# Products on constants around the router and in the first stretch, and new offsets for the order of issue, in a hybrid attention and MoE layer

## The chip, the cores and the metric

The kernel runs on one core of one Trainium2 chip. The metric is the device time in microseconds (us) of one execution. The engines are named as in the profile: PE is TensorE's matmul, PEld its weight load, DVE VectorE, ACT ScalarE, POOL GpSimd, SP SyncE. A name with a q at its end (SPq, ACTq) is the sequencer of that engine where it issues DMAs.

## The reference

One layer of a decoder trunk is computed for 256 tokens of a prompt and for 8 sample sequences with one new token each, all in fp32. The 264 rows are called tokens below.

```python
sh1, sc1, g1, sh2, sc2, g2 = split(silu(c) @ ada_w + ada_b, 6)     # adaLN
h = rms_norm(x, norm1_w) * (1 + sc1) + sh1
z = h @ w_in                       # retention q k v g, attention q k v, indexer q k w
ret_out, ret_state = retention_group(...)        # 8 heads, chunks of 128
att_out = attend(...)              # sparse attention: indexer picks the top keys
x = x + g1 * (concat(ret_out, att_out) @ w_out)
h = rms_norm(x, norm2_w) * (1 + sc2) + sh2
logits = h @ router_w + router_b   # top 4 of 32 experts, softmax over the four
for e in 32 experts:
    hh = h @ w_gate_up[e] + b_gate_up[e]
    gate, up = min(hh[:, :1024], 7), clip(hh[:, 1024:], -7, 7)
    acc += combine[:, e] * (((up + 1) * gate * sigmoid(1.702 * gate)) @ w_down[e] + b_down[e])
x = x + g2 * acc
```

The outputs are the new x of both groups, the new keys, values and indexer keys, and the retention states. The experts' weights are 32 x 12.6 MB; they are by far most of what the kernel reads.

## The kernel before

**The stages.** The program is written as one function. First come the adaLN products (`ada_half`, line 319, and `ada_part`), the statistics of the first norm (line 390) and the scaling of the transposed input (`modulate`, line 401). Then the blocks of w_in are multiplied (line 536 for the prompt, 539 for the sample sequences), and retention and sparse attention are worked out between them. Then comes the projection w_out with the second norm (`norm2`, with transposes at line 268), the router (`router`, products at lines 1340 and 1342), the rank of each token in its expert's list (`ranks`, products at lines 1361 and 1362), the gathers of the first experts' tokens as products with one-hot matrices (`gather_in`, line 1378), and the 32 experts (gate and up at line 1564, down at line 1574).

**The weights.** All large weights go through one queue, SP's (`load`, line 165), in the order in which they are used, into a ring of tiles that holds 21 MB. A tile is loaded again when the last product that reads it is done. When the attention is over, the ring holds the first experts' weights, and the next load waits for expert 0's first four of eight gate and up pieces.

**The order.** Each part of the program is a segment (`seg`). The table `PRIO` gives a segment an offset in the scheduler's priority; the scheduler then puts the instructions of each engine into one fixed order. Segments without an entry stand as written. In each engine the instructions are issued in this order, and one that waits holds up those behind it. `chain()` ties instructions into a given order without a wait between engines.

**The products on constants.** Lines 281 to 283 multiply a 128x128 matrix of ones in bf16 with a broadcast of it, 128x512, twenty times at the start, before the first real product has data. Their result is read by nobody.

**Places that the prediction speaks of.** `ada_half(0)` ends with an addition on DVE (line 327) that the two transposes of `modulate` (line 268) wait for. In the middle stretch, lines 730 and 733 find the threshold of the top keys, line 776 (DVE) and 778 (PE) the row numbers of the keys that are gathered by POOL (line 893), lines 1043 and 1058 the softmax of the prompt's attention, and lines 302, 351 and 1081 fold the second norm's weight (`norm2_w`) into adaLN's rows and transpose them. ACT's queue issues the load of `norm2_w` (line 302), DVE multiplies (line 351), PE transposes (line 1081).

Of the kernel before, what the change touches and what calls it, by code (L numbers as in the profile page):

```python
# [11 lines left out]
F32 = mybir.dt.float32  # L12
# [17 lines left out]

WARM = 20

PRIO = {
# [12 lines left out]
}  # L46


# [70 lines left out]
def hybrid_step(ctx, tc, A, L, O, KP, KT, DEC, poff, toff, dbg=None, stop=None):  # L119
    nc = tc.nc  # L120
    dbg = dbg or {}
    V, S, G, T = nc.vector, nc.scalar, nc.gpsimd, nc.tensor
# [9 lines left out]
    def seg(name):  # L132

        if cur[0] is not None:
            cur[0].__exit__(None, None, None)
        o = PRIO.get(name)
        cur[0] = None
        if o is not None:
            cur[0] = tc.high_priority(offset=o)
            cur[0].__enter__()  # L140
# [125 lines left out]
    def transpose(out, in_):  # L266
        k = in_.shape[0]
        return T.transpose(out, in_, ident[:k, :k])
# [10 lines left out]
    S.dma_start(cr, L["c"])  # L279

    idle = thp()
    for i in range(WARM):
        T.matmul(idle.rearrange("p (n m) -> p n m", n=4), ones_b, ones_b[:, None, :].to_broadcast([128, 4, 128]), start=True, stop=True)

    sw_ = pe.tile([128, 204], F32, name="sw_")
    S.dma_start(sw_, L["small"])
# [34 lines left out]
    def ada_half(h, w):  # L321
        pa = acc()
        for k in range(8):
            for j in range(4):
                T.matmul(pa[32 * j:32 * j + 32, :256], cT[:, k, :], w[k][:, 256 * j:256 * j + 256], start=(k == 0), stop=(k == 7))
        sl = slice(256 * h, 256 * h + 256)
        V.tensor_add(ada[:, 0, sl], pa[:, :256], bias0[:, sl])

# [73 lines left out]
    def modulate(h):  # L402

        seg(f"AB{h}")
        pt = trp()
        for v in range(2):
            transpose(pt[:, 128 * v:128 * v + 128], ada[:, 0, 256 * h + 128 * v:256 * h + 128 * v + 128])
        ptv = pt[:, :256].rearrange("p (v s u r) -> p v s u r", v=2, s=2, u=2)
        qs = slice(2 * h, 2 * h + 2)
        V.tensor_copy(AB[:, qs, 0:64], pt[:, :256].rearrange("p (v m) -> p v m", v=2)[:, :, 0:64])  # L410
        for u in range(2):
            V.scalar_tensor_tensor(Av[:, qs, 1, u], ptv[:, :, 1, u], 1.0,
                                   n1T[:, 4 * h + 2 * u:4 * h + 2 * u + 2, None].to_broadcast([128, 2, 32]), op0=ALU.add, op1=ALU.mult)
        for i in range(4):
            k, u, q = 4 * h + i, i // 2, 2 * h + i % 2
            a_, b_ = AB[:, q, 64 + 32 * u:65 + 32 * u], AB[:, q, 32 * u:32 * u + 1]
            if i % 3 == 1:
                S.activation(hT[:, k, 0:256], hT[:, k, 0:256], AF.Identity, scale=a_, bias=b_)
            else:
                V.tensor_scalar(hT[:, k, 0:256], hT[:, k, 0:256], a_, b_, op0=ALU.mult, op1=ALU.add)  # L420
        hs = hT[:, 4 * h:4 * h + 4, 256:264].rearrange("p (u v) t -> p u v t", u=2)
        for i, op in ((1, ALU.mult), (0, ALU.add)):
            ins = G.tensor_tensor(hs, hs, Av[:, qs, i, :, 1:9].rearrange("p v u r -> p u v r"), op=op)
        if h == 0:
            pool1(ins)
# [7 lines left out]
    gidx = pe.tile([128, 4], I32, name="gidx")  # L433
    V.tensor_copy(gidx, ptf[:, 0:4])
    ikv = A["cache_idx_k"][0].rearrange("n (g k) d -> (n g) (k d)", g=8)
    seg("ikg")
    ikg = []
    for g in range(4):
# [27 lines left out]
    pe1 = chain()  # L466
# [822 lines left out]
    def norm2(c):  # L1289
# [20 lines left out]
        for n in range(2):  # L1310
            sl = slice(512 * n, 512 * n + 512)
            pt = trp()
            for k in range(4):
                transpose(pt[:, 128 * k:128 * k + 128], x[:, c, 512 * n + 128 * k:512 * n + 128 * k + 128])
            o = xT[:, 4 * n:4 * n + 4, 128 * c:128 * c + 128]
            if n:
                V.tensor_copy(o, pt.rearrange("p (k t) -> p k t", k=4))
            else:
                S.activation(o, pt.rearrange("p (k t) -> p k t", k=4), AF.Copy)
            S.activation(hn[:, c, sl], x[:, c, sl], AF.Square, accum_out=ss[:, n:n + 1])  # L1320
# [4 lines left out]
    def norm_rows(c):  # L1325
        seg(f'nr{c}')
        V.tensor_scalar(hn[:, c, 0:512], x[:, c, 0:512], rinv[:, c:c + 1], None, op0=ALU.mult)
        S.activation(hn[:, c, 512:], x[:, c, 512:], AF.Copy, scale=rinv[:, c:c + 1])
# [2 lines left out]
    G.memset(lx, 0.0)  # L1331
    G.memset(selb, 0.0)

    def router(c):
        seg(f'ro{c}')
        rows = 128 if c < 2 else 8
        pl = trp()
        for k in range(8):
            if c < 2:
                T.matmul(pl[:, 0:32], xT[:, k, 128 * c:128 * c + 128], rwm[:, k], start=(k == 0), stop=(k == 7))  # L1340
            else:
                T.matmul(pl[:8, 0:32], h2Ts[:, k], rw_[:, k], start=(k == 0), stop=(k == 7))
        lg = prep.tile([128, 2, NE], F32, name="lg", bufs=3)
# [79 lines left out]
    pr = smp()  # L1423
    ranks(0)
    norm_rows(0)
    norm2(1)
    seg("g0")
    oh0 = [prep.tile([128, D if n == "g1b" else 128], F32, name=n)[:, :112].rearrange("p (x t) -> p x t", x=2) for n in ("ones_f", "g1b")]
    px0 = [slots() for _ in range(2)]
    slot_hits(oh0[0], rankm[:, 0, 0:2])  # L1430
    for g in range(2):
        gather_in(px0[g], oh0[0], 0, g)
    router(1)
    ranks(1)
    norm_rows(1)
    seg("g1")
    slot_hits(oh0[1], rankm[:, 1, 0:2])
    for g in range(2):
        gather_in(px0[g], oh0[1], 1, g)
    seg("smx")  # L1440

    mx = prep.tile([128, 2, 3], F32, name="mx")
# [334 lines left out]
```

## Time and profile before

| | us |
|---|---|
| median of 3 runs | 1259.63 |
| fastest and slowest of them | 1259.60, 1273.12 |
| the profiled execution | 1265.59 |
| its span, first to last instruction | 1263.8 |
| mean granted TensorE clock | 0.977 |
| PE busy | 1177.6 (93%) |
| moved by DMA | 475.81 MB, 454.04 MB of it by the queue of the weights |

A granted clock of 1.00 is TensorE's 2.4 GHz, 0.50 its 1.2 GHz; these are the two levels. In a row of the timeline the first number is the start in us, the second the time that the group took, then engine, line, operation and tiles, the count, and in brackets how long the engine stood idle before it and what released it. In a row of windows stand a stretch, its length, the busy time of each engine with its count, the granted clock, the busy share of the 16 DMA engines, and GB/s.

### The profile page before, as it was taken

The numbers are of one execution on the slowest core, as the hardware profiler recorded it, in microseconds if no ns is written. First come the engines' busy times: TensorE is split into PE (matmuls) and PEld (weight loads), VectorE is DVE, ScalarE is ACT, GpSimd is POOL, SyncE is SP. The second block draws the span as 40 slices with busy tenths as digits, with TensorE's granted clock in tenths as the row PEclk, the third lists the DMA queues.
The fourth block names the chain that finished last, engine by engine and source line by source line (L and its number), as shares of the span: only waits on it lengthen the run. The fifth ranks groups of instructions, "written<-read, shape, count | busy, mean of one in ns | idle before, by whom it ended". The sixth has DMA issues, their size and how long they took to land. (4 is left out here: it accounts for less than half of the span.)

```text
span 1263.8 us, 14203 instructions
## 1 busy us (share of the span) xinstructions
PE 1177.6 (93%) x5661; PEld 471.6 (37%) x5662; DVE 489.3 (39%) x1171; ACT 134.6 (11%) x289; POOL 139.1 (11%) x221
## 2 busy tenths in 40 slices
PE   7999989889999999999999898989999898989898
PEld 3343333356643333433333333333333333333332
DVE  3339865436434333432334233323323332333243
ACT  1222112211210000000000000000000000000000
POOL 3402273340000000000000000000000000000000
PEclk8999999989899999999999999999999999999999
DMA  9636896757769999999999999999999999999997
GB/s 381 266 127 238 296 370 227 236 195 310 305 248 424 430 429 428 429 430 427 431 428 430 429 427 429 431 428 428 429 430 428 430 429 430 427 430 406 428 428 313
DMA packets 53350, 475.81 MB, mean 376 GB/s; under 512 B 6896, under 2 KB 7568, under 8 KB 15520
## 3 DMA queue, kind: packets, MB, share of 16 engines
q1 hardware_dynamic: 45472, 454.04, 85.9%
q0 software_dynamic: 4432, 13.74, 3.0%
q10 hardware_dynamic: 3376, 7.09, 1.9%
q8 instruction: 46, 0.75, 0.2%
q14 instruction: 24, 0.20, 0.0%
HBM read 470.69 MB, written 4.11 MB: 376 GB/s over the span
## 5 line engine op out<-in xcount | busy, mean ns | idle before, releaser
L1564 PE MATMUL pg<-w,xg 128*64 128x512 f32 x2048 | 471.9, 601 | 36.0 <-DMA w<-lay_w_exp 35.4
L1564 PEld LDWEIGHTS pg<-w,xg 128*64 128x64 f32 x2048 | 140.8, 137 | 324.3 <-issue 267.8
L1574 PE MATMUL py<-w,sg 128*64 128x512 f32 x1024 | 234.2, 599 | 12.0 <-DMA w<-lay_w_exp 11.5
L1538 DVE TENSOR_TENSOR hb<-pt,biasT 128x512 f32<-128x512 f32 x64 | 44.3, 692 | 358.1 <-PE pt L1497 349.4
L1523 POOL TENSOR_SCALAR og<-kp,rankm,comb 128x64 f32<-128x64 f32 (+1 forms) x64 | 36.7, 590 | 849.6 <-PE pz L1508 795.2
L1574 PEld LDWEIGHTS py<-w,sg 128*64 128x64 f32 x1024 | 70.8, 137 | 146.4 <-issue 129.2
L1530 ACT ACTIVATE hs<-pg 128x512 f32<-128x512 f32 x64 | 38.2, 597 | 619.9 <-PE pg L1564 619.9
L536 PE MATMUL acc<-w,hT 128*128 128x512 f32 x208 | 103.3, 628 | 0.2 <-DMA w<-lay_w_in 0.2
L1581 DVE TENSOR_TENSOR ys<-py,g2n 64x512 f32<-64x512 f32 x62 | 42.7, 689 | 113.2 <-PE py L1574 112.4
L1508 PE MATMUL pz<-ys,og 128*128 128x512 f32 (+1 forms) x136 | 68.1, 633 | 1.6 <-DVE ys L1577 0.8
L1511 DVE TENSOR_TENSOR x<-x,pz 128x512 f32<-128x512 f32 x68 | 46.5, 687 | 57.3 <-PE pz L1508 57.3
L1378 PE MATMUL pz<-oh,hn 128*128 128x112 f32 x480 | 58.1, 274 | 0.0
L1378 PEld LDWEIGHTS pz<-oh,hn 128*128 128x128 f32 x480 | 56.0, 192 | 0.0
L536 PEld LDWEIGHTS acc<-w,hT 128*128 128x128 f32 x208 | 37.2, 194 | 43.3 <-issue 41.1
L1543 ACT ACTIVATE sg<-hb 128x256 f32<-128x256 f32 x64 | 26.7, 417 | 223.1 <-DVE hb L1542 223.1
L1497 PEld LDWEIGHTS pt<-ident,hs 128*128 128x128 f32 x256 | 26.8, 140 | 52.3 <-issue 52.3
L1497 PE MATMUL pt<-ident,hs 128*128 128x128 f32 x256 | 42.0, 286 | 0.0
L1508 PEld LDWEIGHTS pz<-ys,og 128*128 128x128 f32 (+1 forms) x136 | 23.2, 192 | 46.1 <-issue 29.7
L1560 DVE COPY og<-pt 128x256 f32<-128x256 f32 (+1 forms) x17 | 7.2, 424 | 66.6 <-PE pt L1497 66.6
L1546 DVE TENSOR_TENSOR sg<-sg,hb 128x256 f32<-128x256 f32 x64 | 26.9, 421 | 3.9 <-DVE hb L1545 0.5
L1545 DVE SCALAR_TENSOR_TENSOR hb<-hb 128x256 f32<-128x256 f32 x64 | 27.2, 425 | 2.2
L314 PE MATMUL acc<-w,cT 128*32 128x512 f32 x128 | 25.9, 632 | 0.5 <-ACT t L846 0.5
(459 smaller groups left out, 858.4 us busy)
## 6 DMA issues: line engine op xcount, KB each, us to landing
w<-lay_w_exp SPq DMA_DIRECT2D x130, 2048.0 KB
w<-lay_w_exp SPq DMA_DIRECT2D x122, 1024.0 KB
w<-lay_ada_w SPq DMA_DIRECT2D x20, 1024.0 KB
w<-lay_w_in SPq DMA_DIRECT2D x15, 1024.0 KB
w<-lay_w_out SPq DMA_DIRECT2D x4, 1024.0 KB
s<-qd ACTq DMA_DIRECT2D x4, 512.0 KB
w<-lay_w_exp SPq DMA_DIRECT2D x4, 512.0 KB
hT<-lay_x SPq DMA_DIRECT2D x1, 1152.0 KB
```

The costliest lines, as they stand in the source:

```text
L536: T.matmul(pc[c], hT[:, k, 128 * c:128 * c + 128], w[k], start=(k == 0), stop=(k == 7))
L1378: put(T.matmul(px[:, k, :n, 8:64], hn[:, c, 512 * g + 128 * k:512 * g + 128 * k + 128], oh, start=(c == 0 and k == 0), stop=(c == 1 and k ...
L1497: on_pe(T.transpose(out, in_, ident[:k, :k]))
L1508: on_pe(T.matmul(pz[n], gT[i, 128 * c:128 * c + 128], ys[i, o:o + 512], start=True, stop=True))
L1511: V.tensor_add(x[:, c, sl], x[:, c, sl], pz[n])
L1523: G.tensor_scalar(og[:, c, js], iota2[:, 0:js.stop - js.start], rank(c), gate(c), op0=ALU.is_equal, op1=ALU.mult)
L1530: S.activation(hss[h], pg[h], AF.Copy)
L1538: V.tensor_tensor(hb, pt.rearrange("p (q b t) -> p q b t", q=4, b=2), bias.rearrange("p (b h q) -> p h q b", b=2, h=2)[:, h, :, :, None].t ...
L1545: V.scalar_tensor_tensor(up, up, 1.0, gate_, op0=ALU.add, op1=ALU.mult)
L1564: on_pe(T.matmul(pg[h][64 * b:64 * b + 64, :], xg[:, k, :], w[u][:, 512 * b:512 * b + 512], start=(k == 0), stop=(k == 7)))
L1574: on_pe(T.matmul(py[64 * n:64 * n + 64, :], sgs[k // 4][:, k % 4], w[u][:, 512 * n:512 * n + 512], start=(k == 0), stop=(k == 7)))
L1581: V.tensor_mul(ys[i64, 512 * n:512 * n + 512], py[64 * n:64 * n + 64], g2n[64 * n:64 * n + 64])
```

## The change

The change adds 25 products on constants, each of the form of lines 281 to 283: nine behind the products of `ada_half(0)` and five behind the two transposes of `modulate(0)`, both bound into one chain (`pe0`) with the work around them; and eleven (3, 3, 3 and 2) around the router and the gathers, bound by a chain `pe2` with the transposes of `norm2(1)`, the router's products and the gathers' products. It writes `router(1)` ahead of the first gather. And it gives new offsets to 35 segments in `PRIO`.

```diff
+WARM2 = (3, 3, 3, 2)
 PRIO = {
-    "AB": -400, "AB0": -1600, "AB1": 200, "Sst": 800, "ada0_0": 100, "ada0_1": 0, "ada1_0": -400, "ada1_5": 100, "ada2_0": -800,
+    "AB": -400, "AB0": -1600, "AB1": 200, "Sst": 800, "ada0_0": -100, "ada0_1": 1600, "ada1_0": -400, "ada1_5": 100,
...
     idle = thp()
-    for i in range(WARM):
-        T.matmul(idle.rearrange("p (n m) -> p n m", n=4), ones_b, ones_b[:, None, :].to_broadcast([128, 4, 128]), start=True, stop=True)
+    pe0 = chain()
+
+    def keep_busy(n):
+        for i in range(n):
+            pe0(T.matmul(idle.rearrange("p (n m) -> p n m", n=4), ones_b, ones_b[:, None, :].to_broadcast([128, 4, 128]), start=True, stop=True))
+
+    keep_busy(WARM)
...
+        if h == 0:
+            pe0(ins)
+            seg("wm")
+            keep_busy(9)
...
+            ins = transpose(pt[:, 128 * v:128 * v + 128], ada[:, 0, 256 * h + 128 * v:256 * h + 128 * v + 128])
+            if h == 0:
+                pe0(ins)
...
+    seg("wm")
+    keep_busy(5)
     seg("ikg")
...
+                if c:
+                    pe2(ins)
...
+    pe2 = chain()
+
+    def keep_warm(n, c):
+
+        seg(f"wm{c}")
+        t = pm_.tile([128, 512], F32, name="py")
+        for i in range(n):
+            pe2(T.matmul(t.rearrange("p (n m) -> p n m", n=4), ones_b, ones_b[:, None, :].to_broadcast([128, 4, 128]), start=True, stop=True))
...
-                T.matmul(pl[:, 0:32], xT[:, k, 128 * c:128 * c + 128], rwm[:, k], start=(k == 0), stop=(k == 7))
+                pe2(T.matmul(pl[:, 0:32], xT[:, k, 128 * c:128 * c + 128], rwm[:, k], start=(k == 0), stop=(k == 7)))
...
     norm_rows(0)
+    keep_warm(WARM2[0], 0)
     norm2(1)
+    keep_warm(WARM2[1], 1)
+    router(1)
+    keep_warm(WARM2[2], 2)
     seg("g0")
...
-        gather_in(px0[g], oh0[0], 0, g)
-    router(1)
+        gather_in(px0[g], oh0[0], 0, g, pe2)
+    keep_warm(WARM2[3], 3)
     ranks(1)
...
-        gather_in(px0[g], oh0[1], 1, g)
+        gather_in(px0[g], oh0[1], 1, g, pe2)
```

**PE, from the router to the first expert.** `pt<-rw_,h2Ts` is the router of the sample sequences, `pt<-rwp,mixT` that of the prompt (both halves), `pt<-ident,x` the transposes of `norm2(1)`, `pg<-selb,tri_b` and `pg<-selb,ones_b` the ranks, `pz<-...,hn` the gathers. Before:

```order
L1342 MATMUL pt<-rw__2344,h2Ts 8x32
L1340 MATMUL pt<-rwp,mixT 128x32 x8
L1342 MATMUL pt<-rw__2344,h2Ts 8x32 x7
L268 MATMUL pt<-ident,x 128x128 x8
L1362 LDWEIGHTS tri_b
L1362 MATMUL pg_2542<-selb,tri_b 128x32
L1340 MATMUL pt<-rwp,mixT 128x32 x7
L1361 LDWEIGHTS ones_b
L1361 MATMUL pg_2542<-selb,ones_b 128x32
...
L1378 MATMUL pz<-ones_f,hn 128x2x56 x8
```

With the change, where the products on constants are line 1359 and the lines above are 1369, 1367, 271, 1389, 1388 and 1405:

```order
L271 MATMUL pt<-ident,x 128x128 x8
L1359 LDWEIGHTS ones_b
L1359 MATMUL py<-ones_b 128x512
L1389 LDWEIGHTS tri_b
L1389 MATMUL pg_2556<-selb,tri_b 128x32
...
L1388 LDWEIGHTS ones_b
L1388 MATMUL pg_2556<-selb,ones_b 128x32
L1367 MATMUL pt<-rwp,mixT 128x32 x7
...
L1405 MATMUL pz<-ones_f,hn 128x2x56 x3
```

Three of the eleven stand ahead of the transposes, between products of the router of the sample sequences; three around the first rank; three behind the second half's router; and two between the two gathers. The second half's rank (`tri_b` again) now stands within the first gather, behind its third product, where it stood behind the eighth.

**PE, the middle stretch ahead of the fold's transposes** (`tr<-ident,ada`, line 1081 before and 1097 now). `t_1813` and `t_1827` are the attention weights of the prompt's first half, `acc<-w,hT` and `sm<-w,hT` the products with a block of w_in. Before:

```order
L268 MATMUL th<-ident,s_1502 128x128
L536 MATMUL acc<-w,hT 128x512 x3
L268 MATMUL tr<-ident,t_1813 128x128 x4
...
L1064 MATMUL acc<-t_1840,av 64x128 x4
L314 MATMUL acc<-w,cT 32x512 x7
L1081 MATMUL tr<-ident,ada 128x64 x4
L539 MATMUL sm<-w,hT 32x512 x4
L958 MATMUL th<-av_x,s_1508 128x512
L963 MATMUL th<-kg,s_1508 32x512 x8
```

With the change:

```order
L271 MATMUL th<-ident,s_1516 128x128
...
L552 MATMUL acc<-w,hT 128x512 x8
L555 MATMUL sm<-w,hT 32x512 x4
L974 MATMUL th<-av_x,s_1522 128x512
...
L271 MATMUL tr<-ident,t_1827 128x128 x8
...
L1080 MATMUL acc<-t_1854,av 64x128 x8
L322 MATMUL acc<-w,cT 32x512 x8
L1097 MATMUL tr<-ident,ada 128x64 x4
```

The block's products, those for the sample sequences (line 539, now 555) with them, moved ahead of the transposes of the attention weights and of adaLN's products (line 314, now 322).

**ACT in the same stretch.** `t_1779` (now `t_1793`) is the copy of what those products for the sample sequences give, `t_1840` (now `t_1854`) that of the transposed attention weights. Before:

```order
L998 ACTIVATE rows<-acc 128x512
L1058 ACTIVATE t_1840<-tr 128x512
L544 ACTIVATE t_1779<-sm 128x512
L302 DMA t_1877<-lay_norm_w 128x512
L1012 DMA s_1794<-vd 64x2x512 x2
```

With the change:

```order
L1014 ACTIVATE rows<-acc 128x512
L1059 ACTIVATE t_1827,st<-t_1827,st 128x128
L560 ACTIVATE t_1793<-sm 128x512
L310 DMA t_1891<-lay_norm_w 128x512
L1074 ACTIVATE t_1854<-tr 128x512 x2
L1028 DMA s_1808<-vd 64x2x512 x2
```

The load of `norm2_w` still follows the copy of the sample products, and both moved ahead of the copies of the transposed attention weights.

The order of SP's loads is the same in both.

## Rows read from the trace of the kernel before

**Rows 1.** Windows of the expert stage: busy time by engine, clock, DMA share, GB/s.
```profile
370.00:420.00 50.00, 49.81 (x216) 17.89 (x216) 19.96 (x37) 2.96 (x6) 2.24 (x4) 0.97 1.00 422
800.00:1240.00 440.00, 402.93 (x1864) 150.12 (x1862) 136.82 (x277) 30.41 (x60) 16.23 (x28) 0.99 1.01 427
```

**Rows 2.** Waits of SP's queue: total us, how many, longest.
```profile
SPq L165 <- PE pg L1564: 128.3, 40, 20.9
```

**Rows 3.** Windows from the router to the first experts.
```profile
333.10:336.30 3.20, 2.93 (x36) 2.69 (x36) 1.91 (x7) 0.72 (x2) 0.00 (x0) 1.00 1.01 417
336.30:353.40 17.10, 16.25 (x71) 13.40 (x71) 8.32 (x39) 2.97 (x5) 4.64 (x10) 0.50 0.52 218
344.60:355.90 11.30, 10.45 (x42) 6.16 (x42) 4.80 (x17) 0.00 (x0) 3.11 (x5) 0.61 0.05 18
```

**Rows 4.** Timeline of PE from the router to the first expert.
```profile
333.26 1.97 PE L1340 MATMUL pt<-rwp,mixT 128*128 128x32 f32 x16
336.01 1.72 PE L268 MATMUL pt<-ident,x 128*128 128x128 f32 x8 [0.27 <-DVE lg L1347]
337.60 3.18 PE L1340 MATMUL pt<-rwp,mixT 128*128 128x32 f32 x14
341.07 3.73 PE L1378 MATMUL pz<-ones_f,hn 128*128 128x112 f32 x16
345.65 2.90 PE L1378 MATMUL pz<-g1b,hn 128*128 128x112 f32 x12 [0.82 <-DVE g1b L1371]
350.33 1.12 PE L1564 MATMUL pg<-w,xg 128*64 128x512 f32 x2
```

**Rows 5.** Timeline of weight loads of expert 0, and the first load on SP's queue.
```profile
352.07 0.26 PEld L1564 LDWEIGHTS pg<-w,xg 128*64 128x64 f32 x2 [0.59 <-issue]
352.92 0.26 PEld L1564 LDWEIGHTS pg<-w,xg 128*64 128x64 f32 x2 [0.59 <-issue]
...
354.45 0.15 PEld L1564 LDWEIGHTS pg<-w,xg 128*64 128x64 f32 x2 [0.28 <-issue]
354.88 0.15 PEld L1564 LDWEIGHTS pg<-w,xg 128*64 128x64 f32 x2 [0.28 <-issue]
...
355.51 3.76 SPq L165 DMA_DIRECT2D w<-lay_w_exp  x2
```

**Rows 6.** Timeline of weight loads for the twenty products on constants.
```profile
4.50 0.15 PEld L283 LDWEIGHTS <-ones_b 128*128 128x128 bf16 x1 [0.28 <-issue]
4.93 0.15 PEld L283 LDWEIGHTS <-ones_b 128*128 128x128 bf16 x1 [0.28 <-issue]
5.29 1.61 PEld L283 LDWEIGHTS <-ones_b 128*128 128x128 bf16 x8 [0.22 <-issue]
```

**Rows 7.** Timeline of the first stretch: PE, POOL, PE.
```profile
21.50 0.41 PE L268 MATMUL tr<-ident,ada 128*128 128x128 f32 x2 [2.80 <-DVE ada L327]
43.39 0.59 POOL L489 TENSOR_TENSOR tc<-kt,sw__157 128x192 f32<-128x192 f32 x1 [1.07 <-DMA kt<-const_t]
50.89 0.33 PE L268 MATMUL tr<-ident,t 128*128 128x128 f32 x1 [1.82 <-POOL t L600]
```

**Rows 8.** Timeline of the middle stretch.
```profile
142.16 0.24 PE L733 MATMUL th<-ce,tri_b 128*128 128x144 bf16 x1 [0.99 <-DVE ce L730]
213.85 0.34 ACTq L302 DMA_DIRECT2D t<-lay_norm_w  x1
221.51 0.68 DVE L351 SCALAR_TENSOR_TENSOR ada<-ada,t 64x512 f32<-64x512 f32 x1 [4.14 <-issue]
222.34 0.43 PE L1081 MATMUL tr<-ident,ada 64*128 64x64 f32 x4 [2.79 <-DVE mixT L971]
```

**Rows 9.** Windows of the middle stretch.
```profile
170.00:222.30 52.30, 42.58 (x250) 16.94 (x246) 33.37 (x86) 10.88 (x30) 23.92 (x27) 0.93 0.77 274
205.00:211.00 6.00, 6.00 (x40) 2.88 (x41) 4.66 (x8) 1.68 (x3) 0.00 (x0) 1.00 0.14 12
223.70:227.10 3.40, 3.40 (x5) 0.95 (x3) 0.00 (x0) 0.00 (x0) 2.64 (x3) 0.50 0.94 320
```

More of the change, by code (lines that the diff above doesn't have):

```diff
@@ L31 @@
 WARM = 20
+WARM2 = (3, 3, 3, 2)
 PRIO = {
[12 rows of a table removed]
[10 rows of a table added]
+    "sa_w10": -1600, "sa_w11": -20, "si_g0": 200, "si_k": 400, "si_n": 1600, "si_q": -20, "si_s": 800, "smx": 800, "st": 1600,
+    "st2": 1600, "wm": 400, "wo": 200, "z0": -1600, "z1024": -100, "z1536": -400, "z2048": 50, "z2560": 50, "z3072": 100,
+    "z3584": 100, "z512": 200, "zik": 200, "ziq": 1600,
 }
@@ L324, in ada_half @@
             for j in range(4):
-                T.matmul(pa[32 * j:32 * j + 32, :256], cT[:, k, :], w[k][:, 256 * j:256 * j + 256], start=(k == 0), stop=(k == 7))
+                ins = T.matmul(pa[32 * j:32 * j + 32, :256], cT[:, k, :], w[k][:, 256 * j:256 * j + 256], start=(k == 0), stop=(k == 7))
+        if h == 0:
+            pe0(ins)
+            seg("wm")
+            keep_busy(9)
         sl = slice(256 * h, 256 * h + 256)
@@ L406, in modulate @@
         for v in range(2):
-            transpose(pt[:, 128 * v:128 * v + 128], ada[:, 0, 256 * h + 128 * v:256 * h + 128 * v + 128])
+            ins = transpose(pt[:, 128 * v:128 * v + 128], ada[:, 0, 256 * h + 128 * v:256 * h + 128 * v + 128])
+            if h == 0:
+                pe0(ins)
         ptv = pt[:, :256].rearrange("p (v s u r) -> p v s u r", v=2, s=2, u=2)
@@ L1313, in norm2 @@
             for k in range(4):
-                transpose(pt[:, 128 * k:128 * k + 128], x[:, c, 512 * n + 128 * k:512 * n + 128 * k + 128])
+                ins = transpose(pt[:, 128 * k:128 * k + 128], x[:, c, 512 * n + 128 * k:512 * n + 128 * k + 128])
+                if c:
+                    pe2(ins)
             o = xT[:, 4 * n:4 * n + 4, 128 * c:128 * c + 128]
```

20 rows, old and new, of the table PRIO are left out of this document.

## The prediction

> **What bounds the kernel now.** I read the windows of the whole span first, then the waits of SP's queue, then the timeline of PE in the stretches where the clock or the DMA share is low. In the expert stage the busy share of the DMA engines is 1.00 to 1.01, at 422 and 427 GB/s, from 370 us to 1240 us [rows 1]. PE is 403 us busy in the last 440 us there, so it isn't what sets the pace: the weights that are still to come, divided by the rate at which they come, give the time from the moment when the stream starts again. That moment is found in the waits: SP's longest wait for a gate and up product is 20.9 us [rows 2], and it ends at 355.51 us, where SP issues its first load after the pause [rows 5]. Ahead of it lies a hole: from 344.6 to 355.9 us the DMA share is 0.05 [rows 3], because every tile of the ring is full and none is given back before expert 0 has used the first one. So a microsecond by which expert 0's first tile is used up earlier moves the stream, and with it the end, by a microsecond. Whatever lies ahead of that counts if it is on PE's path to expert 0; whatever lies behind it, in the expert stage, is covered by the stream.
>
> The second thing that the windows show is the clock. From 336.3 to 353.4 us the granted clock is 0.50, which is TensorE's 1.2 GHz, while PE was busy for 16.25 of 17.10 us [rows 3]. In the 3.2 us ahead the clock was 1.00 and PE was busy for 2.93 us [rows 3], with products of 32 columns [rows 4]. So the clock fell there while PE did many small products, not in a wait: the longest idle time in that place is 0.27 us [rows 4].
>
> **The change, part by part.**
>
> *Router and first gathers.* At the full clock 16 products of the router take 1.97 us, 0.123 us each; at the low one 14 take 3.18 us, 0.227 us each [rows 4]: a ratio of 0.54. From 336.30 us to expert 0's first product at 350.33 us PE spends 14.03 us, of which 0.82 us are a wait [rows 4]. If the clock stays at 1.00, the 13.2 us of work become 7.1 us, a gain of 6.1 us. The eleven added products cost 1.61 / 8 = 0.20 us each at the full clock [rows 6], together 2.2 us. The wait of 0.82 us for the second one-hot matrix I leave as it is, although the second rank is now issued earlier. A new wait is possible ahead of the second half's norm, where ACT now has four small DMA issues in front of it; an issue on ACT's queue takes 0.34 us [rows 8], so 1.4 us, and I let 0.4 us of it show, as PE has the router's products in that place. So expert 0 starts 6.1 - 2.2 - 0.4 = 3.5 us earlier.
>
> Then the first tile: eight pairs of products. At the low clock the weight loads of a pair stand 0.85 us apart (352.07, 352.92), at the full clock 0.43 us (354.45, 354.88) [rows 5]. Before, the eight took from 350.33 to 355.51 us, 5.2 us; at the full clock they take 8 x 0.43 = 3.4 us. That is another 1.7 us (1.74 unrounded), so **5 us** for this part.
>
> Its bounds: at best the 0.82 us go as well, 6 us. At worst the clock falls as before and stays down. Then each of the eleven products costs 0.43 us (weight loads at 4.50 and 4.93 us, in the low clock of the start [rows 6]), 4.7 us together; the 0.4 us of the new wait show; and four of the eight pairs, which ran at 0.43 us, run at 0.85 us, 1.7 us: 6.8 us lost. I take the gain, since the added products stand between exactly those small products in which the clock fell, and the row nearest to them, eight of their kind in 1.61 us [rows 6], shows the clock up while only such products ran.
>
> The Trainium skill speaks against this: its page "TensorE: Matmul & The Clock Gate", section "HAM oscillation — how this bites in real kernels", has the clock fall in gaps in which PE stands idle, in waits on DMA. By that rule there was nothing here for the products to fill, and they would only add their time. The trace disagrees with it as far as it goes, since no gap stands ahead of this fall.
>
> *First stretch.* The fourteen products there are put where PE waits 2.80 us for DVE's addition [rows 7] and where it waits again behind the transposes. They lie in idle time: nine cost 1.8 us and five 1.0 us at the full clock. I cost them, and what the clock gains from them, at nothing, as PE is not what the next step waits for: the table of constants lands only in time for POOL's first step at 43.39 us, and PE waits 1.82 us for POOL at 50.89 us [rows 7]. A PE that is faster before that waits longer there. If that cover were gone, PE's gain would be seen; since PE issues in order and waits for POOL, I leave only 0.6 us for it, one of POOL's steps of 0.59 us [rows 7]. If the nine run at 0.43 us, 3.9 us for a gap of 2.8 us, the transposes come 1.1 us later. So 0, with bounds of -0.6 and +1 us.
>
> *Middle stretch.* The new offsets change the order there. Three rows are to go. The threshold's product waits 0.99 us for DVE [rows 8]; its segment now comes later in PE's order, behind products that are ready. The fold's transposes wait 2.79 us [rows 8]: the row names line 971, but DVE's step before it, line 351, ran at 221.51 us after 4.14 us with no wait on an engine, on the `norm2_w` that ACT issued only at 213.85 us [rows 8]. Now the copy that stands ahead of this issue, and the sample products that it copies, come before adaLN's last products, thus some 5 us earlier, in a stretch where the DMA share was 0.14 [rows 9]. And the clock falls to 0.50 behind that wait, from 223.7 to 227.1 us [rows 9]: half of 3.4 us, 1.7 us. Together 0.99 + 2.79 + 1.7 = 5.5 us.
>
> Against it: between 170 and 222.3 us PE stood idle for 52.3 - 42.6 = 9.7 us [rows 9], 6.9 us of it in other waits than the fold's. The new order moves a block's products of w_in ahead of the softmax's transposes, and puts off DVE's steps on the gathered keys behind one-hots; this closes some of these waits and opens others (transposes of the sample scores and of the attention weights have less work in front of them). I take these 6.9 us as unchanged, less half a us that I choose to put on the exponentials, which ACT now does later: **5 us**. Bounds: if a fifth of the 6.9 us goes too, 7 us of gain; if the fold's wait and the low clock stay and three hand-overs of the price of the threshold's (0.99 us) are new, 3.0 - 1.0 = 2 us of loss.
>
> *Moved past by nothing.* SP's loads keep their order, and the added products use no queue but PE's own. `router(1)` ahead of the first gather moves eight products of the router, 1 us, ahead of work that was to follow anyway: 0.
>
> The sum is 0 - 5 - 5 = -10 us. It is made against the profiled execution of 1265.59 us (span 1263.8), and gives 1255.6 us. That execution is 5.96 us above the median of the runs, so against the median of 1259.63 us I say **1250 us** (1249.6).
>
> **The rivals.**
>
> *Only one of the two parts works* (the middle waits come back at other places, or the clock recovers only halfway to expert 0). For it speaks that two gains of 5 us each rest on separate reasons, and that the 6.9 us of other waits are only estimated. Against it: both have rows of their own. 1259.6 - 5 = 1254.6 us, from 1251 to 1259.
>
> *The clock stays low through the router, slower.* The eleven products then cost 6.8 us and give nothing back. Place: between the prompt's first router product and expert 0's first product. It decides when the granted clock is still 0.50 where the first gather starts. With the middle's 5 us it gives 1259.6 + 6.8 - 5 = 1261.4 us, from 1259 to, without the middle's gain, 1268. For it speaks that between the added ones there still stand small products and transposes, the very work in which the clock fell [rows 4], and that the wait of 0.82 us is left. The rule of the Trainium skill's section named above leads to this case too. Against it: the added ones stand in four places among them, so that no long run of small ones is left.
>
> *The change doesn't do what it says:* the first tile's release is set by something that comes after PE, or the stream makes up for its start, and the time stays at 1259.6 us. Against it: the load is issued at 355.51 us, right behind the eighth pair, and the share of 1.00 afterwards leaves nothing to make up with [rows 1, 5].
>
> **How the numbers follow.** Both parts as forecast: 0.52, 1250 us; its own range is 1246 to 1255 us, from all the bounds of gain (6 + 7 + 0.6 = 13.6 us) to half of the forecast (10 us) gone. Only one: 0.24. Clock stays low: 0.18. No effect: 0.06. The range of 1246 to 1263 us takes in the first, second and fourth case and about three fifths of the third; what is left out is the rest of that case and a little below. Two per cent, about what a measurement of this kernel can tell from no change, are 25 us: no case reaches 1234.4 or 1284.8 us, and I leave 0.03 to each side for what I haven't seen, 0.94 for within.
>
> **What would show it.** Right, if in the profile after the granted clock is 1.00 from the router to the first expert, expert 0's first product comes some 8.5 us earlier than 350.33 us (5 by the middle, 3.5 by the router), and SP's first load some 10 us earlier than 355.51 us, with the DMA share still 1.00 from 370 us on. The middle is right if the fold's transposes don't wait and the clock is 1.00 behind them; the first stretch if PE still waits for POOL at about 50 us. I am wrong if the clock falls again in the router's stage, if new waits of PE between 170 and 222 us exceed 7 us, or if the stream starts earlier and the end doesn't follow.

## The result, and the profile after

The changed kernel is slower, by less than one per cent: a median of 1273.2 us (1269.62 to 1278.76, 20 runs) against 1265.69 us (1255.85 to 1273.12, 20 runs) of the kernel before, a ratio of 1.0066 with a 95% interval of 1.0047 to 1.0085. By that ratio, which is not quite that of the two medians (they lie 7.5 us apart), it is 8.3 us more (6 to 11); 10 us less were forecast, and the range ended at 1263 us. The profiled execution took 1272.24 us, its span is 1270.5 us.

What the forecast said of the end holds. In the windows of the changed kernel the stream of weights runs as before, at the same share and rate [rows 1]:

```profile
420.00:800.00 380.00, 370.17 (x1758) 140.75 (x1754) 126.60 (x259) 28.38 (x56) 15.67 (x28) 1.00 1.01 429
800.00:1240.00 440.00, 404.10 (x1864) 151.22 (x1864) 136.80 (x277) 30.41 (x60) 16.90 (x30) 0.99 1.01 427
```

What the forecast said of the router holds too, for this execution. The timeline of PE in the changed kernel (columns as in [rows 4]; 1369 was 1342, 1367 was 1340, 271 was 268, 1405 was 1378, 1595 was 1564):

```profile
345.67 0.23 PE L1369 MATMUL pt<-rw__2358,h2Ts 128*8 128x32 f32 x2
345.82 1.97 PE L1367 MATMUL pt<-rwp,mixT 128*128 128x32 f32 x16
...
349.63 1.09 PE L271 MATMUL pt<-ident,x 128*128 128x128 f32 x8 [0.27 <-DVE lg L1374]
...
353.00 0.81 PE L1359 MATMUL py<-ones_b 128*128 128x512 bf16 x3
...
357.45 1.12 PE L1405 MATMUL pz<-g1b,hn 128*128 128x112 f32 x8
358.71 6.66 PE L1595 MATMUL pg<-w,xg 128*64 128x512 f32 x30
```

From the router's first product to expert 0's it takes 358.71 - 345.67 = 13.0 us, where it was 350.33 - 333.11 = 17.2 us, and SP issues its first load 3.7 us later, not 5.2 us as in [rows 5] (the row of SP's queue in the changed kernel: first line below; behind it the windows of the router's stretch and of the first tile, clock 1.00 in both, against 0.50 in [rows 3]):

```profile
362.39 3.76 SPq L168 DMA_DIRECT2D w<-lay_w_exp  x2
```

```profile
345.70:358.70 13.00, 12.61 (x107) 10.45 (x107) 8.38 (x39) 3.70 (x7) 1.71 (x6) 1.00 0.93 386
358.70:362.30 3.60, 3.59 (x18) 1.55 (x20) 1.66 (x6) 0.00 (x0) 3.05 (x5) 1.00 0.01 2
```

But the router begins at 345.67 us and not at 333.11 us, 12.6 us later. Up to the sample state's products (`th<-s,qb`) PE is where it was: 259.29 us now, 259.18 us before. The time is lost between, in a stretch of which neither the forecast nor its rivals say a word: the prompt's retention, from the first product of its scores (`acc<-s,qkT`) to the first product `pz<-w,mixT` of the projection. In the kernel before it reads, in the timeline of PE:

```profile
290.13 1.75 PE L836 MATMUL acc<-s,qkT 64*128 64x128 f32 x16
292.16 0.41 PE L1149 MATMUL acc<-rows,t 128*128 128x64 f32 x2 [0.28 <-DVE t L1143]
292.49 1.49 PE L836 MATMUL acc<-s,qkT 64*128 64x128 f32 x16
293.91 1.77 PE L1149 MATMUL acc<-rows,t 128*128 128x64 f32 x14
...
315.21 7.03 PE L1275 MATMUL pz<-w,mixT 128*128 128x512 f32 x16
```

In the changed kernel (852 was 836, 1165 was 1149, 1291 was 1275), with the windows of the whole stretch and of the low clock in it:

```profile
289.49 1.75 PE L852 MATMUL acc<-s,qkT 64*128 64x128 f32 x16
291.52 0.41 PE L1165 MATMUL acc<-rows,t 128*128 128x64 f32 x2 [0.28 <-DVE t L1159]
291.85 0.93 PE L852 MATMUL acc<-s,qkT 64*128 64x128 f32 x6
292.71 0.43 PE L1165 MATMUL acc<-rows,t 128*128 128x64 f32 x2
293.08 0.48 PE L852 MATMUL acc<-s,qkT 64*128 64x128 f32 x2
293.49 0.43 PE L1165 MATMUL acc<-rows,t 128*128 128x64 f32 x2
...
296.97 0.79 PE L852 MATMUL acc<-s,qkT 64*128 64x128 f32 x2
297.69 0.69 PE L1165 MATMUL acc<-rows,t 128*128 128x64 f32 x2
...
305.17 3.25 PE L1165 MATMUL acc<-rows,t 128*128 128x64 f32 x14
...
310.25 13.44 PE L1291 MATMUL acc<-w,mixT 128*128 128x512 f32 x26
...
327.26 7.03 PE L1291 MATMUL pz<-w,mixT 128*128 128x512 f32 x16
```

```profile
289.50:327.30 37.80, 37.52 (x142) 23.71 (x141) 17.82 (x42) 3.53 (x7) 1.82 (x3) 0.73 0.54 213
293.60:314.10 20.50, 20.50 (x73) 14.10 (x74) 8.01 (x19) 2.53 (x4) 0.00 (x0) 0.51 0.56 225
```

The stretch takes 37.77 us, where it took 25.08 us: 12.7 us more. With the 4.2 us that the router's stretch gains, the 1.7 us of the first tile and 0.1 us in all the rest, that is the whole difference of the two profiled spans (1270.5 - 1263.8 = 6.7 us). Two things differ in the stretch. The scores' products of the second half stand one by one between the output's products of the first, where they stood in a row; and the granted clock is at its low level, 1.2 GHz, for 20.5 us, in all of which PE is busy.

### The profile page after: what moved, and what is told of

Same layout as the page of the kernel before. It is cut to its first block, busy times and chain, and to the rows that moved or that the text cites. A ratio compares the mean times of both kernels' runs of the same rounds, so it can differ in the third digit from the quotient of the medians.

```text
span 1270.5 us, 14257 instructions
## 1 busy us (share of the span) xinstructions
PE 1193.9 (94%) x5686; PEld 480.9 (38%) x5687; DVE 491.9 (39%) x1171; ACT 134.9 (11%) x289; POOL 139.1 (11%) x221
## 5 line engine op out<-in xcount | busy, mean ns | idle before, releaser
L552 PE MATMUL acc<-w,hT 128*128 128x512 f32 x208 | 99.8, 614 | 0.0
L322 PE MATMUL acc<-w,cT 128*32 128x512 f32 x128 | 25.2, 633 | 2.9 <-issue 2.9
```

Of the source, the lines that this page charges most:

```text
L552: T.matmul(pc[c], hT[:, k, 128 * c:128 * c + 128], w[k], start=(k == 0), stop=(k == 7))
```

## The experiments

Theory A: the new order of the retention's products costs the time (A1 through the clock, A2 by itself). Theory B: the clock falls there by where the stretch happens to start in time, and the order has no part in it. A further question goes with them: what the forecast's other three parts are worth, each alone. All ratios are to the kernel before, with the 95% interval; "the stretch" is the retention's as above. Of the table `PRIO` the cuts of code show only the entries that change, not its whole lines.

**e1**, the change with the old order of the retention alone put back (`ro0` and `ro1` name both the retention's output and the router in the table, so the former gets a name of its own):

```diff
-        seg(f'ro{c}')
+        seg(f'rp{c}')
...
-    "gn0": 20,
+    "gn0": 50, "rp0": -50, "rp1": -800,
```

> The changed kernel, with the prompt's retention products (in1, output of both halves, their norm) put back under the offsets of the kernel before (-50, -800, 50, under names of their own); all else of the change stays. Theory A, the new order there costs: in the changed kernel the stretch from the first in1 product to the first pz product of the projection takes 37.8 us, before 25.1 us; this should go back to 25 to 26 us, with the granted clock 1.00 in it, and the time 10 to 12 us below the changed kernel, a ratio of 0.997 to the kernel before. Theory B, the clock falls there by where the stretch happens to start in time, whatever the order: the stretch stays above 32 us at 0.50, the ratio stays near 1.006.

Measured 1.0008 (0.9986 to 1.0031), 12 runs. The window of the stretch shows the clock at 1.00:

```profile
294.70:319.70 25.00, 24.21 (x141) 15.34 (x140) 17.89 (x42) 3.53 (x7) 1.82 (x3) 1.00 0.76 307
```

The stretch is back at 25.08 us, and most of the loss is gone with it, so A. The 0.997 that A asked for lies below the interval; the same kernel once more (e14) gave 0.9974.

**e2**, the change without the eleven products.

```diff
-WARM2 = (3, 3, 3, 2)
+WARM2 = (0, 0, 0, 0)
```

> The changed kernel without its eleven products around the router and the gathers. If they hold the clock (forecast and theory A): the clock is 0.50 between the router and expert 0 again, that stretch takes 17 us where it takes 12.9 us with them, and the time is 4 to 6 us above the changed kernel, ratio 1.010. If they only cost time: 2.2 us less than the changed kernel, ratio 1.005, the clock 1.00 there without them too.

Measured 1.0097 (1.0071 to 1.0123), 6 runs: 0.003 above the changed kernel, at the lower end of what the forecast said, and hardly clear of the two intervals. The trace shows why it is less: without the products the router's stretch takes 13.97 us, not 17, with the clock at 0.88.

```profile
354.30:368.30 14.00, 11.97 (x98) 11.05 (x98) 8.96 (x40) 3.70 (x7) 3.10 (x8) 0.88 0.87 365
```

**e3**, the change without the first stretch's fourteen products.

```diff
-            seg("wm")
-            keep_busy(9)
...
-    seg("wm")
-    keep_busy(5)
```

> The changed kernel without the nine and the five products of the first stretch. Forecast and theory A: no change, ratio 1.006, as PE waits for POOL at 50 us either way (longer with the products). Theory B: the clock falls elsewhere afterwards, and the time moves by several us either way.

Measured 1.0119 (1.0092 to 1.0147), 6 runs: 0.005 above the changed kernel, which the forecast had not. In its trace PE reaches the threshold's product at 142.85 us, the changed kernel at 142.98 us, so it isn't lost in the first stretch. It reaches `th<-s,qb` 2.0 us later (261.33 us). Open until e13 and e14.

**e4**, the change with the `PRIO` of before (the lines of the diff above on that table undone): products and calls stay.

> The changed kernel with the whole table of offsets of the kernel before: all added products and the order of the calls stay. Theory A: retention back in its old order, router at full clock: 4 to 6 us below the kernel before, ratio 0.996. If the other new offsets (middle stretch) bring what was forecast, it is slower than e1 by 5 us; if they bring nothing, the same as e1. Theory B: ratio 1.000 to 1.006.

Measured 0.9986 (0.9968 to 1.0005), 12 runs, the stretch at 25.08 us. It is 0.002 below e1, not above it, and 0.001 above e14, which is the same kernel as e1: no gain of 5 us from the other new offsets shows.

**e5**, the kernel before with the retention's new order alone.

```diff
-        seg(f'ro{c}')
+        seg(f'rp{c}')
...
-    "gn0": 50,
+    "gn0": 20, "rp0": 20, "rp1": 400,
```

> The kernel before with one part of the change alone: the prompt's retention products under the new offsets (output of the halves 20 and 400, norm 20, under names of their own). Theory A: from the first in1 product to the first pz product 37.8 us in place of 25.1 us, 12.7 us more, with the clock at 0.50 for some 20 us there; the time 12 us above the kernel before, ratio 1.010. Theory B (the clock falls there by where the stretch starts): in this kernel nothing ahead of the stretch differs from before, so it stays at 25 us and the ratio at 1.000.

Measured 1.0084 (1.0048 to 1.0120), 9 runs: this one part gives the whole loss. In its windows the low clock stands as in the changed kernel, 20.5 us long, though nothing ahead of the stretch differs from the kernel before:

```profile
289.90:327.80 37.90, 37.62 (x141) 23.36 (x140) 17.97 (x42) 3.53 (x7) 1.84 (x3) 0.73 0.65 248
294.90:315.40 20.50, 20.50 (x71) 13.41 (x71) 8.01 (x19) 3.04 (x5) 0.00 (x0) 0.51 0.61 249
```

Theory B falls.

**e6**, the kernel before with the first stretch's products alone (the diff's two hunks on `ada_half` and `modulate`, and the one ahead of `ikg`).

> The kernel before with the nine and the five products of the first stretch alone (the products of the first norm's statistics move a little with them). Forecast: nothing, ratio 1.000, since PE waits for POOL at 50 us. If the 6 us by which e3 is slower than the changed kernel are due to these products: ratio 0.995. If they cost time by the clock's later falls (the search's products stood 3 to 5 us later in the traces of e1, e2 and e4): ratio 1.003.

Measured 0.9977 (0.9951 to 1.0002), 12 runs: no difference that it can tell. The router's stretch in its trace is a surprise. There are no products on constants there, and still it takes 12.06 us, with the clock at 1.00:

```profile
329.70:341.70 12.00, 10.28 (x96) 9.30 (x95) 8.65 (x39) 3.70 (x7) 2.03 (x6) 1.00 1.00 406
```

**e7**, the kernel before with the eleven products and the early `router(1)` alone.

> The kernel before with the eleven products around the router and the gathers and router(1) ahead of the first gather, nothing else. Forecast: the stretch from the router to expert 0 at clock 1.00 in 13 to 14 us in place of 17.2, the time 5 us below before, ratio 0.996. If the products only trade their own time against the clock: 1.000.

Measured 1.0002 (0.9976 to 1.0028), 12 runs, with the router's stretch at 14.07 us under its old offsets. The forecast's 0.996 is outside of the interval: over these runs this part gains nothing.

**e8**, the changed kernel once more.

> The changed kernel once more, for its time beside the others on one chip and for a second trace. Ratio 1.0066 as before, and the retention stretch again 37 to 38 us with the clock at 0.50, if theory A holds; under theory B the fall of the clock stands elsewhere in a second execution.

Measured 1.0073 (1.0047 to 1.0099), 11 runs. The stretch takes 37.86 us in this second trace, with the low clock again for 20.5 us from 292.1 us, so A as in e5.

**e9**, e5 with twelve products on constants among the retention's output products, bound to them by a chain.

```diff
         po = acc()
+        if c == 0:
+            pe3, hold = chain(), trp()
         for h in range(8):
-            T.matmul(po[:, 64 * h:64 * h + 64], inn[:, h], rv[:, c, 64 * h:64 * h + 64], start=True, stop=True)
+            pe3(T.matmul(po[:, 64 * h:64 * h + 64], inn[:, h], rv[:, c, 64 * h:64 * h + 64], start=True, stop=True))
+            if c == 0 or h % 2:
+                pe3(T.matmul(hold.rearrange("p (n m) -> p n m", n=4), ones_b, ones_b[:, None, :].to_broadcast([128, 4, 128]), start=True, stop=True))
```

> e5 (the kernel before with the new retention order) with twelve products on constants put between the retention's output products. If the clock's fall is what makes the stretch long (theory A1): the clock stays 1.00, the stretch takes 25.1 + 2.4 for the added products + some 2 us for products that no longer stand in pairs, 29 to 30 us, against 37.8 us in e5; ratio 1.003. If the order itself costs the time, at either clock (theory A2): 38 us or more, ratio 1.010.

Measured 1.0048 (1.0018 to 1.0078), 12 runs. The windows of the stretch, and of the one fall of the clock that is left in it:

```profile
295.40:325.70 30.30, 30.02 (x156) 18.87 (x152) 18.03 (x42) 3.53 (x7) 1.83 (x3) 0.94 0.84 324
302.30:305.70 3.40, 3.40 (x15) 2.90 (x15) 1.15 (x2) 0.00 (x0) 0.00 (x0) 0.56 1.00 422
```

30.3 us is close to what A1 asked for (29 to 30), though the clock isn't 1.00 throughout. Of the 12.7 us the clock is thus some 10 us: the products add 2.4 us, and 30.3 - 2.4 = 27.9 us are left of 37.9. The 2.8 us that remain above 25.1 are the order itself and the last 3.4 us at the low clock (1.7 us of them). An estimate from e5 alone gives the clock about as much: 20.5 us at half the clock are at most 10.3 us longer than at the full one. It leaves at least 2.5 us to the order, more than the 1.1 us of e9, in which the products on constants stand between.

**e10**, e5 with only the first half's offset.

```diff
-    "gn0": 20, "rp0": 20, "rp1": 400,
+    "gn0": 50, "rp0": 20, "rp1": -800,
```

> e5 with the second half's offsets put back (output -800, norm 50): only the first half's output products are mixed with in1's. If the mixing is what lets the clock fall: the stretch stays at 36 us or more, ratio 1.008. If it needs the later place of the second half's output too: 27 to 30 us, ratio 1.002.

Measured 1.0056 (1.0031 to 1.0080), 7 runs; the stretch takes 37.22 us:

```profile
295.60:332.80 37.20, 36.92 (x143) 23.90 (x140) 18.09 (x42) 3.53 (x7) 1.83 (x3) 0.72 0.66 258
```

Mixing the two kinds of product is what does it; where the second half's output stands matters little.

**e11**, e1 with the diff of e3; **e12**, e6 with twelve products behind the transposes of `rq_s`.

```diff
-    transpose(pt[:, 0:128], rq_s)
+    pe4 = chain()
+    pe4(transpose(pt[:, 0:128], rq_s))
+    for i in range(12):
+        pe4(T.matmul(pt[:, 128:512].rearrange("p (n m) -> p n m", n=3), ones_b, ones_b[:, None, :].to_broadcast([128, 3, 128]), start=True, stop=True))
```

> e1 (the changed kernel with the retention's old order) without the fourteen products of the first stretch. If these bring 3 to 6 us, as e6 and e3 against the changed kernel say: ratio 1.004 to 1.006, against 1.0008 of e1. If they bring nothing (forecast): 1.001.

> e6 (the kernel before with the first stretch's products) with twelve products on constants, 384 columns each, behind the transposes of rq_s, where PE waited 2.42 us for DVE; the sample state's products (qb) then come later in the order, behind part of rgr's. Meant as the best version: ratio 0.996 if both bring something, 0.998 as e6 if only the first stretch's do.

Measured 0.9932 (0.9906 to 0.9957), 6 runs, for e11, and 0.9982 (0.9960 to 1.0005), 12 runs, for e12. e11 contradicts e3: there the same fourteen products seemed to gain 0.005, here they seem to cost 0.008. e12 brings nothing over e6.

**e13** and **e14**, e11 and e1 once more on one chip, and **e15**, e11 with the diff of e2 as well.

> e11 once more (the changed kernel, retention's old order, no products in the first stretch). If the first stretch's products cost time: ratio 0.993 again, 0.007 below e14. If what set e11 apart is where the clock happened to fall in those executions: nearer to 0.998, and e14 no longer apart from it.

> e1 once more, beside e11 on one chip (the same but for the fourteen products). If they cost time: 1.001, 0.007 above e13. If the clock's falls set the two apart: within 0.003 of e13. In both traces the arrival of PE at the sample state's products (rs2) should follow 252.5 + 0.40 x the time at the low clock between 58 us and there, within 2 us, as in the thirteen traces so far.

> e11 without the eleven products around the router as well: of the change only the other offsets and the order of the calls are left. If the router's products hold a clock that else falls in most executions: 0.004 above e13. If the clock falls there only in some, as the 12.06 us of that stretch without them in e5 and e6 say: the same as e13 or up to 0.0015 below.

Measured, 12 runs each: 0.9994 (0.9969 to 1.0018) for e13, 0.9974 (0.9951 to 0.9997) for e14, 0.9979 (0.9960 to 0.9999) for e15. What set e11 apart doesn't come again, and with the products (e14) the time is not above the one without (e13). So the fourteen products do nothing that these runs can tell. e15 lies 0.0015 below e13, which is no difference that these intervals can tell, so the router's products hold nothing worth 0.004 there. None of these versions is faster than the kernel before by a margin worth the name; of the two that were run twice, e11 and e13 gave 0.9932 and 0.9994, e1 and e14 1.0008 and 0.9974.

e11 and e13 are one kernel, and their intervals don't meet: the intervals are too narrow for what differs between one set of runs and the next, and a difference of less than about 0.006 between two versions is not shown by one set each. The retention's order stands clear of this: the seven sets with the new order (the changed kernel, e2, e3, e5, e8, e9, e10) lie from 1.0048 to 1.0119, the nine with the old one from 0.9932 to 1.0008.

The rule for the arrival at `th<-s,qb` (252.5 us and 0.40 us for each us at the low clock since 58 us) gave 265.8, 262.3 and 264.2 us for e13, e14 and e15, by the rounded clock of the windows; measured 265.96, 262.94 and 266.60 us. The last is 0.4 us beyond the 2 us that were allowed. (How the rule is worked out stands in the last section.)

## Why the prediction was wrong

**What sets the end: right.** In the sixteen traces other than that of the kernel before, the span ends 911.7 to 912.1 us after expert 0's first product; before it is 1263.8 - 350.33 = 913.5 us, since its first tile ran in part at the low clock. That is the forecast's 1.7 us, measured 1.4 to 1.8 us. Every microsecond ahead of expert 0 came out at the end.

**The base: 6 us too low.** The forecast was made against the median of three runs, 1259.63 us; the median of twenty is 1265.69 us, so the profiled execution of 1265.59 us lay in the middle of the runs and not 5.96 us above it. Of the 23.6 us between 1249.6 and 1273.2 us, 6.1 are this, 10 the gain that didn't come, and 7.5 the loss.

**The step that failed: the sum has no term for the retention.** The forecast took the new offsets for a matter of the stretch from 142 to 262 us. The order of PE also changes between 290 and 300 us, and the sum holds nothing for it, not even a zero with a cover. It is 12.7 us (37.8 against 25.1), shown alone by e5 and undone by e1. None of the prediction's own signs of being wrong came: they look at the router, at the waits up to 222 us and at the stream's start. The two parts of the 12.7 us could have been bounded from the trace of before. The clock: the forecast had seen, at the router, that it falls while PE is busy with small products, and the new order makes a longer run of just such products. The order itself: in a row, eight scores' products take 1.49 us (16 records), 0.19 us each; between others one takes 0.41 us (293.08 to 293.49 in the changed kernel, still at the full clock) and an output product 0.37 us (292.71 to 293.08) in place of 0.25.

A rule of the Trainium skill bears on the order: its page "TensorEngine Tiling (Array Packing)", section "Tiling Modes", says that products in different tiles of the array run in parallel, and that a change of the tiling mode drains the engine. The scores use 64 rows of the array, the output 128, and the trace agrees: 0.19 against 0.41 us. The runs don't tell the two effects apart, nor do they show why the clock falls in the mixed order.

**The middle stretch: 5 us forecast, none measured.** The mechanism came as described: the fold's transposes don't wait, at 217.46 and 221.75 us, and the clock behind them is 1.00:

```profile
217.46 0.46 PE L1097 MATMUL tr<-ident,ada 64*128 64x64 f32 x4
...
221.75 0.46 PE L1097 MATMUL tr<-ident,ada 64*128 64x64 f32 x4
```

```profile
217.50:228.00 10.50, 10.50 (x54) 5.42 (x50) 3.38 (x8) 0.00 (x0) 6.78 (x7) 1.00 0.94 338
```

What was mis-sized is the work itself, which the forecast had taken as unchanged. From 58 us to `th<-s,qb` PE is 185.1 us busy and 16.2 us idle, before 179.8 and 21.4 us, in stretches of the same length and rounded clock:

```profile
58.00:259.30 201.30, 185.13 (x941) 77.54 (x938) 133.31 (x407) 42.13 (x103) 66.28 (x81) 0.97 0.71 255
```

```profile
58.00:259.20 201.20, 179.78 (x933) 74.15 (x932) 130.42 (x407) 41.09 (x103) 66.39 (x81) 0.97 0.70 252
```

So in this pair 5.2 us of waits went, as forecast, and 5.3 us of work came. The groups by line show where (of the changed kernel, then of before):

```profile
L555 PE MATMUL sm<-w,hT 128*32 128x512 f32 x100 | 19.0, 622 | 0.0
L979 PE MATMUL th<-kg,s 128*32 128x512 f32 x32 | 7.0, 636 | 0.0
L794 PE MATMUL th<-pay,s 128*128 128x4 bf16 x64 | 5.1, 168 | 2.0 <-DVE s L792 2.0
```

```profile
L539 PE MATMUL sm<-w,hT 128*32 128x512 f32 x96 | 15.7, 640 | 0.0
L963 PE MATMUL th<-kg,s 128*32 128x512 f32 x32 | 4.9, 599 | 0.0
L778 PE MATMUL th<-pay,s 128*128 128x4 bf16 x64 | 3.7, 167 | 1.5 <-issue 1.0 <-DVE s L776 0.5
```

They take 6.8 us more, with about as many records and about the same mean of one (other groups take less: the prompt's products `acc<-w,hT` 90.4 us where they took 94.2); the new order has cut their groups. Four products 32 columns wide take 1.06 us together, and one of them alone takes 1.05 us (a cut group of the changed kernel, then a whole one):

```profile
147.44 1.05 PE L555 MATMUL sm<-w,hT 128*32 128x512 f32 x2
...
148.65 1.06 PE L555 MATMUL sm<-w,hT 128*32 128x512 f32 x6
...
209.53 1.06 PE L555 MATMUL sm<-w,hT 128*32 128x512 f32 x8
```

That the cuts eat the gain is read from these two traces, and in the same size from e8 against e6 (the four groups with `th<-qkn,qx` 30.5 and 25.2 us); no run undoes the cuts alone. The sixteen traces in which the order up to `th<-s,qb` can be compared (all but e12) say the same with a smaller size: from 58 us to that product PE is idle for 18.4 to 21.4 us with the old offsets and for 15.9 to 18.2 us with the new ones, and `sm<-w,hT` takes 14.8 to 16.6 us with the old and 18.0 to 19.5 us with the new. A least-squares fit through them, with the time at the low clock taken from windows of 5 us, puts the new offsets, at equal time at the low clock, at 3.2 us less idle time, 3.7 us more work, and an arrival 0.4 us later (give or take 0.6). So the waits were worth some 3 us rather than 5, and the middle gains nothing; e4 beside e1 and e14 shows no gain either.

**The router: right for the profiled execution, not for the median.** Forecast were 3.5 us up to expert 0's first product; the traces show 17.2 to 13.0, 4.2 us. But the price of before was taken from one execution in which the clock had fallen there. Of the eight traces without the eleven products, six pass that stretch in 12.06 to 12.45 us at the full clock (e5, e6, e9, e10, e12, e15), one in 13.97 us (e2), and only the one of before in 17.2. With the products it is 13.0 to 14.1 us in all nine. So where the clock stays up they cost 0.6 us under the new offsets (13.06 us in e13, 12.45 us in e15, whose window stands here) and 2.0 us under the old ones (14.07 us in e7, 12.06 us in e6); where it falls they gain, 4.2 us against the trace of before and 0.9 us against e2. That fits e7 at 1.0002.

```profile
340.20:352.70 12.50, 10.48 (x98) 9.51 (x97) 8.93 (x40) 3.70 (x7) 3.07 (x8) 1.00 0.97 401
```

The worst case of this part took its price of 0.43 us for a product on constants from 4.50 us, as one at the low clock; the profile has the granted clock at 1.00 there (before, window 4.00 to 5.00 us). The price itself holds: at the clock of 0.50 in e9 one takes 0.43 us from start to start (303.46 to 303.89 us).

On the rule that was set against this part: the section "HAM oscillation — how this bites in real kernels" of the Trainium skill's page "TensorE: Matmul & The Clock Gate" would have the products do nothing, as no gap stands there. Here the trace disagrees: e9 held the clock, but for 3.4 us, with such products in a run of small ones, in which e5 shows it low for 20.5 us with PE busy for all 20.5 us.

**The first stretch: right.** PE waits for POOL until 50.43 us in the changed kernel (50.89 us before [rows 7]), and e3, e6, e11, e13 and e14 together show no effect of one sign.

```profile
50.43 0.33 PE L271 MATMUL tr<-ident,t 128*128 128x128 f32 x1 [3.66 <-POOL t L616]
```

**The difference of 8.3 us** is then 12.7 us of the retention, and 0 for each of the forecast's parts. The 4 us between are within the intervals (e5 alone: 6 to 15 us), and I can't split them further: e1 and e14, the whole change but the retention's order, are at +1 and -3 us.

## What to carry to other kernels

List every place where an order of issue changed, also those that no wait marks, and price the work in the new order, not only its waits: products that use a part of the array's rows or columns are cheap only beside their like. A low clock in one trace is the price of that execution; look at a second trace of the same program, or at the clock of its other runs, before a gain is built on it. In this kernel a run of small products in mixed shapes is where the clock fell with PE fully busy, and twelve products on constants among them held it for most of the time, at their own price.

## What the runs showed of the hardware

The clock stood at 1.2 GHz for 20.5 us while PE was busy all the time, in the five traces with the retention's new order and no products added to it (the changed kernel, e2, e3, e5, e8), and likewise in e10; in none of the ten with the old order does it fall in that stretch. In the changed kernel the low clock lasted into the first products of 512 columns behind it, which begin at 310.25 us, until 314.1 us.

Executions of one program differ by where else the clock falls. The changed kernel's two traces show it low for about 12 and 8 us between 58 us and `th<-s,qb` (by the clock of the windows, 0.97 and 0.98: length x (1 - clock) / 0.5), and reach that product at 259.29 and 256.05 us; e5 (0.96) reaches it at 258.83 us, e1 (0.94) at 263.75 us, e2 (0.92) at 266.88 us. From e8 to e2 that is 25 us more at the low clock and 10.8 us later. Over thirteen traces (before, changed, and e1 to e11), from 256.05 to 266.88 us, the arrival follows the time at the low clock by about 0.40 us for each us, within 2.2 us, whatever the offsets.

This bears on why 20 runs of the kernel before lie between 1255.85 and 1273.12 us, and a run without a profile shows it too, by its mean clock. Over the 107 runs of the kernel before that stand beside e1 to e15, the time at the low clock, worked out from that mean in the same way, goes from 38 to 89 us, and the span rises with it by 0.31 us for each us (correlation 0.93). So most of what differs between executions of this one program goes with its time at the low clock; why the clock falls more often in some is not shown.
